# Hybrid attention layer on one core: earlier queries for the memory heads, halved loads for the sparse attention, a shorter preparation lead in the output product

## The chip, the core and the metric

The kernel runs on one core of a Trainium2 chip. The core has a matrix engine (TensorE, PE in the profile), VectorE (DVE), ScalarE (ACT), GpSimd (POOL), and SyncE (SP), whose queue issues the loads and stores. All five run their own list of instructions in order and wait for each other through semaphores; 16 DMA engines move data between main memory and the on-chip memory. The metric is the device time of one execution in microseconds (us).

## The reference

One layer on a sequence of 1024 tokens of width 2048. One projection feeds three groups of attention heads: multi-head latent attention (MLA, 8 heads), native sparse attention (NSA, 4 heads, with compressed, selected and window branches) and cross-attention to a memory of 256 tokens (4 heads). Everything is float32.

```python
def hybrid_layer(x, mem, cos, sin, norm_g, w_in, q_norm_g, w_uq, kv_norm_g, w_ukv,
                 cmp_pe_k, cmp_pe_v, cmp_w1k, cmp_w2k, cmp_w1v, cmp_w2v,
                 mem_norm_g, w_mem_kv, w_out):
    h = rmsnorm(x, norm_g) @ w_in
    offsets = np.cumsum(IN_SPLITS)[:-1].tolist()
    (c_q, c_kv, k_rope, z_mla, q_nsa, k_c, v_c, k_s, v_s, k_w, v_w, g_nsa, z_nsa,
     q_mem, z_mem) = jnp.split(h, offsets, axis=-1)
    o_mla = mla_mixer(c_q, c_kv, k_rope, cos, sin, q_norm_g, w_uq, kv_norm_g, w_ukv) * jax.nn.silu(z_mla)
    o_nsa = nsa_mixer(q_nsa, k_c, v_c, k_s, v_s, k_w, v_w, g_nsa,
                      cmp_pe_k, cmp_pe_v, cmp_w1k, cmp_w2k, cmp_w1v, cmp_w2v) * jax.nn.silu(z_nsa)
    o_mem = memory_mixer(q_mem, mem, mem_norm_g, w_mem_kv) * jax.nn.silu(z_mem)
    o = jnp.concatenate([o_mla, o_nsa, o_mem], axis=-1) @ w_out
    return x + o.astype(x.dtype)
...
    return rmsnorm(x, final_norm_g)
```

## The kernel before

Every float32 operand of the large products is split into a rounded high part and a remainder (`split`, L118 on ScalarE and L112 on VectorE), and `mm3` multiplies high by high, high by low and low by high (L124 to L126): three matmuls of 128x512 for one block.

**Stages.** Up to about 100 us the inputs are normalised. Up to 1000 us the projection runs: 40 units `u` of 7 products `s` each (a product scheme with 7 block products in place of 8), so products g = 7u + s; one product is 12 matmuls. After each product its bank is drained (`evac`), and from the second half on (u >= 20) GpSimd adds the first half's result with an accumulating DMA (work<-part). `post` finishes a unit: for the gate tiles a Silu on ScalarE (L795) and a store. From 1000 us come the four NSA heads (row blocks i = 0 to 7 of 128 tokens), up to about 1557 us the eight MLA heads, and then the output product and the final norm.

**Side work in the projection.** `at(u, s, f)` puts a piece of other work behind product (u, s): the compression of the NSA keys and values (chunks that pass through wh buffers), the memory heads (`mem_start`, `mem_scores`, ...) and, in unit 39, the loads for NSA (`nsa_keys`, `nsa_window`, `nsa_aux`, `nsa_values_in`, `nsa_masks`). There TensorE, VectorE, ScalarE and GpSimd keep the order of the program text; SP's order comes from a scheduler. In the NSA and MLA heads a scheduler orders all engines by priority.

**Memory heads.** Head h has its first scores at product 64 + 18h of the second half. `mem_start` (four products ahead) loads its queries (qh, ql: two wh buffers, 512 KB each) and its keys and values (km, vm into one rs buffer).

**Output product.** 56 products t of 24 matmuls, in seven phases p = t // 8 with k = t % 8. `w_load` and `a_load` bring weights (into a wraw buffer) and entries (ogT, into work buffers); `w_prep` splits the weights into a big buffer, `a_prep` adds or subtracts entries where the phase wants it (L1497, L1501) and splits the sum into a wh buffer. At the end of each phase `oevac` drains the eight PSUM banks into row buffers Y: on VectorE as sums (L1616 after the third phase, L1622 after the fourth). In phases 1, 3 and 5 the products go on in the banks of the phase before. `oside` does the residual, the squares of the norm (L1575), GpSimd's product with the norm's gain (L1651) and, in the last phase, row outputs: `inverse` (L1580 to L1587) and `scaled_out` (L1595 on VectorE). The last four products are done row by row, so that rows 4 to 7 can be finished one by one: there every row needs all of the four.

**Buffers.** big 16, wh 8, work 4, wraw 3, rs 2; PSUM banks S 4, T 2, O and J 2 together. In the output product gf, the eight Y and the four S1 and S2 hold 13 of the big buffers, so three are left for split weights. All of this part, from the gain's load on, keeps the order of the program text on the four engines:

```python
    for t in range(NT):
        p, k = divmod(t, 8)
        if t + 4 < NT:
            w_load(t + 4)
            a_load(t + 4)
        if t + 3 < NT:
            w_prep(t + 3)
            a_prep(t + 3)
```

Behind these lines stand the 24 matmuls of product t, then the drain where k is 7, then `oside(p, k)`.

Of the kernel before, what the change touches and what calls it, by code (L numbers as in the profile page):

```python
# [52 lines left out]
def hybrid_block_kernel(ctx: ExitStack, tc, a, out):  # L53
# [607 lines left out]
    mem = {}  # L661

    def mem_start(h):
        qh, ql = whl()
        load(f(qh), qmd[h][:, :1024])
        load(f(ql), qmd[h][:, 1024:])
        kv = rs()
# [4 lines left out]
        mem[h] = (qh, ql, kv)  # L672
# [115 lines left out]
    def post(u, n):  # L788
# [5 lines left out]
        elif j >= T_ZMLA:  # L794
            S.activation(o, o, AF.Silu)  # L795
# [198 lines left out]
    for h in range(4):  # L994
        g = 64 + 18 * h
        at(u0 + (g - 4) // 7, (g - 4) % 7, lambda h=h: mem_start(h))
# [9 lines left out]
    at(ul, 0, lambda: nsa_keys())  # L1006
    at(ul, 1, lambda: nsa_window())
    at(ul, 3, lambda: nsa_aux())
    at(ul, 4, lambda: nsa_values_in())
    at(ul, 6, lambda: nsa_masks())  # L1010

# [12 lines left out]
    def nsa_window():  # L1024
        kw = big()
        nsa["kwm"] = (kw[:, :1024], kw[:, 1024:])
        load(f(kw), kwd)
        kw = big()
        kw1, kw2 = nsa["kw"] = kw[:, :1024], kw[:, 1024:]
        for r0 in (0, 64):  # L1030
            load(f(kw1[r0:r0 + 64]), kswh[64:])
        load(f(kw2[:64]), kswl[64:])
        load(f(kw2[64:]), posd[:, 64:])

    def nsa_values_in():
        nsa["vs"], nsa["vw"] = big(), big()
        load(f(nsa["vs"]), vsd)
        load(f(nsa["vw"]), vwd)

    def nsa_keys():  # L1040

        kh, kl, k1, k2 = [slot() for _ in range(4)]
        nsa["ks"] = (kh, kl), k1, k2
        load(f(kh[:, :64]), kcd[:, :64])
        load(f(kl[:, :64]), kcd[:, 64:128])
        load(f(k1[:, :64]), kcd[:, 128:192])
        load(f(k2[:64, :64]), kcd[:64, 192:])
        load(f(kh[:, 64:]), ksd[:, :1024])
        load(f(kl[:, 64:]), ksd[:, 1024:])
        for r0 in (0, 64):  # L1050
            load(f(k1[r0:r0 + 64, 64:]), kswh[:64])
        load(f(k2[:64, 64:]), kswl[:64])
        load(f(k2[64:]), posd)
# [26 lines left out]
    post(2 * NU - 1, 0)  # L1080
    post(2 * NU - 1, 1)
# [326 lines left out]
    for h in range(4):  # L1408
        q = qn
        for i in range(8):  # L1410
# [5 lines left out]
            src = nsa_scores(h, q, i)  # L1416
            if h == 3 and i == 7:
                ckv.extend(latent(4))
# [68 lines left out]
    def a_prep(t, dst=None):  # L1487
# [8 lines left out]
        if p == 2:  # L1496
            V.tensor_tensor(s1, r[0], r[1], op=ALU.add)  # L1497
            V.tensor_tensor(s2, s1, r[2], op=ALU.subtract)
            src = s2
        elif p == 3:  # L1500
            V.tensor_tensor(r[0], r[0], r[1], op=ALU.subtract)  # L1501
            src = r[0]
        elif p == 4:
            src = s1
        elif p == 5:
            V.tensor_tensor(s2, r[0], s2, op=ALU.subtract)
            src = s2
        else:
            src = r[0]
# [306 lines left out]
```

## Time and profile before

| | us |
|---|---|
| three runs | 1887.09, 1892.62, 1897.51 |
| median | 1892.62 |
| the profiled execution | 1892.9 |
| its span, first to last instruction | 1891.1 |
| TensorE busy | 1786.8 (94%) |
| VectorE busy | 1317.0 (70%) |
| ScalarE busy | 854.9 (45%) |
| GpSimd busy | 323.8 (17%) |
| mean granted clock of TensorE | 0.979 |

A wait is given with the engine that idled, the line and tiles of the instruction that waited, and the instruction or transfer that came last by the profile. Where an instruction waits for several, the one named need not be the one that mattered. The granted clock is TensorE's share of full speed: 1.00 is 2.4 GHz, 0.50 is 1.2 GHz.

### The profile page before, as it was taken

How to read it: one execution, taken by the hardware profiler on the slowest of the kernel's cores; microseconds unless marked ns; L12 is line 12 of the kernel's file. 1: busy time of each engine (PE TensorE's matmuls, PEld its weight loads, DVE VectorE, ACT ScalarE, POOL GpSimd, SP SyncE). 2: the span in 40 equal slices, each digit the busy share in tenths (PEclk: the TensorE clock that was granted, in tenths of full speed). 3: DMA queues.
4: the chain of work that ended last, by engine and by line, in shares of the span. 5: the costliest groups of instructions: out<-in, count | busy, mean ns of one | idle time of the engine just before them, and what ended most of it. 6: DMA issues, size and time to landing. Idle time of an engine off the chain costs nothing. (4 is left out here: it accounts for less than half of the span.)

```text
span 1891.1 us, 26430 instructions
## 1 busy us (share of the span) xinstructions
PE 1786.8 (94%) x9294; PEld 1523.0 (81%) x9294; DVE 1317.0 (70%) x2478; ACT 854.9 (45%) x1712; POOL 323.8 (17%) x433
## 2 busy tenths in 40 slices
PE   8999999999999999999997999999999999989996
PEld 7888878887777777877776898888998988877885
DVE  7976878976866655666564887868778783454777
ACT  8754222222434344544555665545455453222344
POOL 0002322323233313233231222200000000000020
PEclk9999999999999999999998999999999999999998
DMA  6554877786678657978998233432122144654564
GB/s 220 187 189 165 286 263 267 253 298 237 225 211 255 161 173 231 293 214 243 307 265 242 68 97 109 167 114 62 46 77 64 57 154 150 226 167 145 172 194 191
DMA packets 124930, 351.91 MB, mean 186 GB/s; under 512 B 15355, under 2 KB 39613, under 8 KB 121725
## 3 DMA queue, kind: packets, MB, share of 16 engines
q1 hardware_dynamic: 119037, 329.25, 51.7%
q0 software_dynamic: 5760, 20.97, 6.3%
q8 instruction: 73, 1.20, 0.3%
q14 instruction: 60, 0.49, 0.1%
HBM read 242.14 MB, written 108.02 MB: 185 GB/s over the span
## 5 line engine op out<-in xcount | busy, mean ns | idle before, releaser
L124 PE MATMUL S<-big,wh 128*128 128x512 f32 x1336 | 528.7, 396 | 25.2 <-DVE work L772 8.3
L125 PE MATMUL S<-big,wh 128*128 128x512 f32 x1336 | 525.7, 393 | 4.4 <-DVE big L112 4.4
L126 PE MATMUL S<-big,wh 128*128 128x512 f32 x1336 | 525.3, 393 | 1.3 <-DVE wh L112 1.2
L124 PEld LDWEIGHTS S<-big,wh 128*128 128x128 f32 x1336 | 254.0, 190 | 82.0 <-issue 12.5
L125 PEld LDWEIGHTS S<-big,wh 128*128 128x128 f32 x1336 | 254.3, 190 | 56.7 <-DVE big L112 5.9
L126 PEld LDWEIGHTS S<-big,wh 128*128 128x128 f32 x1336 | 253.6, 190 | 56.9 <-DVE wh L112 3.0
L112 DVE TENSOR_TENSOR wh<-wraw,wh 128x512 fp32r<-128x512 f32 (+2 forms) x226 | 199.0, 882 | 73.8 <-ACT wh L118 73.6
L118 ACT ACTIVATE wh<-wraw 128x512 fp32r<-128x512 f32 (+2 forms) x226 | 145.4, 659 | 90.4 <-PE S L126 44.2
L112 DVE TENSOR_TENSOR big<-wraw,big 128x1024 fp32r<-128x1024 f32 x56 | 73.9, 1320 | 105.1 <-ACT big L118 100.5
L733 POOL TENSOR_TENSOR wraw<-wraw 128x512 f32<-128x512 f32 x38 | 56.6, 1488 | 459.6 <-DMA wraw<-in_w_feat 394.6
L659 ACT ACTIVATE work<-S,st 128x512 f32<-128x512 f32 (+3 forms) x148 | 84.6, 573 | 86.5 <-DVE st L1114 35.1
L118 ACT ACTIVATE wh<-rs 128x512 fp32r<-128x512 f32 x80 | 50.2, 628 | 157.7 <-POOL rs L734 125.6
L112 DVE TENSOR_TENSOR wh<-rs,wh 128x512 fp32r<-128x512 f32 x80 | 63.0, 787 | 65.5 <-ACT wh L118 65.4
L118 ACT ACTIVATE big<-wraw 128x1024 fp32r<-128x1024 f32 x56 | 59.2, 1056 | 85.6 <-PE J L126 59.4
L124 PE MATMUL J<-big,wh 128*128 128x512 f32 x214 | 84.1, 393 | 0.8 <-ACT wh L118 0.7
L125 PE MATMUL J<-big,wh 128*128 128x512 f32 x214 | 84.0, 393 | 0.0
L126 PE MATMUL J<-big,wh 128*128 128x512 f32 x214 | 83.9, 392 | 0.0
L118 ACT ACTIVATE wh<-T 128x512 fp32r<-128x512 f32 (+2 forms) x112 | 53.0, 504 | 45.6 <-PE T L1179 29.5
L770 ACT ACTIVATE work<-S 128x512 f32<-128x512 f32 x40 | 23.9, 597 | 106.7 <-PE S L126 99.2
L112 DVE TENSOR_TENSOR wh<-T,wh 128x512 fp32r<-128x512 f32 (+2 forms) x112 | 61.5, 569 | 10.6 <-ACT wh L118 10.3
L1443 POOL MEMSET wh<- 128x128 f32 x64 | 13.8, 228 | 291.8 <-PE O L125 173.6
L1096 PE MATMUL S<-big,big 128*128 128x512 f32 (+2 forms) x144 | 52.9, 367 | 9.7 <-ACT wraw L659 9.7
(378 smaller groups left out, 4132.1 us busy)
## 6 DMA issues: line engine op xcount, KB each, us to landing
wraw<-in_w_feat SPq DMA_DIRECT2D x80, 512.0 KB, 5.5
part<-work SPq DMA_DIRECT2D x40, 512.0 KB, 3.7
work<-part POOLq DMA_DIRECT2D x40, 512.0 KB, 6.4
work<-og SPq DMA_DIRECT2D x72, 256.0 KB, 4.0
wh<-in_w_o SPq DMA_DIRECT2D x32, 512.0 KB, 7.2
t<-wh SPq DMA_DIRECT2D x32, 512.0 KB, 3.0
wraw<-t SPq DMA_DIRECT2D x32, 512.0 KB, 3.7
wraw<-in_w_o SPq DMA_DIRECT2D x24, 512.0 KB, 3.9
```

Of the source, the lines that this page charges most:

```text
L112: V.tensor_tensor(dst, src, f(hi), op=ALU.subtract)
L118: S.activation(hi, src, AF.Copy)
L124: PE.matmul(dst, sh, mh, start=start, stop=False, skip_group_check=shared)
L125: PE.matmul(dst, sh, ml, start=False, stop=False, skip_group_check=shared)
L126: PE.matmul(dst, sl, mh, start=False, stop=stop, skip_group_check=shared)
L659: S.activation(dst, src, AF.Exp, bias=m, scale=-1.0, accum_out=s)
L733: E.tensor_tensor(B12, B22, B12, op=ALU.subtract)
L770: S.activation(C21, B, AF.Copy)
L1096: PE.matmul(d, qm[0][:, c:c + P], km[0][:, k0:k0 + n], start=True, stop=False)
L1443: G.memset(f(t[:, o:o + P]), 0.0)
```

## The change

1. The memory heads' query loads move from four to eight products ahead of the head's first scores; keys and values stay at four (`mem_kv`).
2. The loads for NSA are split into two halves of columns and begin two products earlier; the masks (cmask, cm01, vc) and their copy come behind the first half of the keys and ahead of the window. All second halves come last.
3. The Silus of the last unit leave the end of the projection and stand in NSA head 0 behind the scores of blocks 1 and 2, at that place of ScalarE's order.
4. In the output product, weights and entries are split two products ahead in place of three; entries are still added up three ahead (`a_sum` and `a_split` in place of `a_prep`).
5. In the third phase (p = 2) the low halves of rows 0 to 3 are squared and multiplied by the gain; in the last phase only the high half is squared, and the low half's scaling is done on ScalarE.

The diff, cut to its core:

```diff
     def mem_start(h):
...
+        mem[h] = qh, ql
+
+    def mem_kv(h):
         kv = rs()
...
-        mem[h] = (qh, ql, kv)
+        mem[h] += kv,
...
-    def post(u, n):
+    def post(u, n, pin=False):
...
-            S.activation(o, o, AF.Silu)
+            x = S.activation(o, o, AF.Silu)
+            if pin:
+                tc.keep_in_program_order(x)
             store(zd[j - T_ZMLA], o)
...
-        at(u0 + (g - 4) // 7, (g - 4) % 7, lambda h=h: mem_start(h))
+        at(u0 + (g - 8) // 7, (g - 8) % 7, lambda h=h: mem_start(h))
+        at(u0 + (g - 4) // 7, (g - 4) % 7, lambda h=h: mem_kv(h))
...
-    at(ul, 0, lambda: nsa_keys())
-    at(ul, 1, lambda: nsa_window())
-    at(ul, 3, lambda: nsa_aux())
-    at(ul, 4, lambda: nsa_values_in())
-    at(ul, 6, lambda: nsa_masks())
+    at(ul - 1, 6, lambda: nsa_keys(0))
+    at(ul, 0, lambda: nsa_aux())
+    at(ul, 1, lambda: nsa_window(0))
+    at(ul, 3, lambda: nsa_values_in(0))
+    at(ul, 5, lambda: nsa_masks(), lambda: nsa_keys(1), lambda: nsa_window(1), lambda: nsa_values_in(1))
...
+    def nsa_window(n):
+        if n == 0:
+            nsa["w"] = big(), big()
+        km, kr_ = nsa["w"]
...
+        c = slice(512 * n, 512 * n + 512)
+        load(halves(f(km))[:, :, c], halves(kwd)[:, :, c])
         for r0 in (0, 64):
...
+            load(f(kw1[r0:r0 + 64, c]), kswh[64:, c])
+        load(f(kw2[:64, c]), kswl[64:, c])
+        load(f(kw2[64:, c]), posd[:, 64 + 512 * n:576 + 512 * n])
...
-    post(2 * NU - 1, 0)
-    post(2 * NU - 1, 1)
...
             src = nsa_scores(h, q, i)
+            if h == 0 and i in (1, 2):
+                post(2 * NU - 1, i - 1, True)
...
-    def a_prep(t, dst=None):
+    asrc = {}
+
+    def a_sum(t):
...
+    def a_split(t, dst=None):
         e = slot()[:, :1024] if dst is None else dst
-        split(e[:, :512], e[:, 512:], src)
+        split(e[:, :512], e[:, 512:], asrc.pop(t))
         ent[t] = e
...
+        if p == 2 and k < 4:
+            square(Y[k][:, L_], st_(k, 0))
+            G.tensor_tensor(Y[k][:, L_], Y[k][:, L_], gf[:, L_], op=ALU.mult)
...
             if k < 4:
-                square(Y[k][:, L_], st_(k, 0))
                 square(Y[k][:, H_], st_(k, 1))
             if 0 < k <= 4:
                 r = inverse(k - 1, 2)
-                scaled_out(k - 1, r, L_)
+                scaled_out(k - 1, r, L_, True)
                 scaled_out(k - 1, r, H_)
...
+        if t + 2 < NT:
+            w_prep(t + 2)
+            a_split(t + 2)
         if t + 3 < NT:
-            w_prep(t + 3)
-            a_prep(t + 3)
+            a_sum(t + 3)
```

What moves on the engines is shown at three places. The first is ScalarE where NSA begins. A line number is followed by the operation, what it writes and what it reads; wraw with st is an exponential's result with its sum, rs from wraw is the copy of the masks, work from work a Silu. Before:

```order
L659 ACT_TABLE_LOAD
L659 ACTIVATE wraw_8102,st_8100<-S_8109,st_8100 128x128
L1063 ACTIVATE rs_8040<-wraw_8041 128x576
L795 ACT_TABLE_LOAD
L795 ACTIVATE work_7965<-work_7965 128x1024
L795 ACTIVATE work_7966<-work_7966 128x1024
L659 ACT_TABLE_LOAD
L659 ACTIVATE wraw_8102,st_8100<-S_8103,st_8100 128x64
```
In the changed kernel, behind the head's first eight exponentials (L798 is a Silu, L1175 the scaling of a branch, L118 a split):

```order
L1175 ACTIVATE wraw_8142<-wraw_8142,st_8140 128x256
L798 ACT_TABLE_LOAD
L798 ACTIVATE work_7980<-work_7980 128x1024
L118 ACTIVATE big_8170<-T_8174 128x3x128
L659 ACT_TABLE_LOAD
L659 ACTIVATE wraw_8182,st_8180<-S_8189,st_8180 128x384
L118 ACTIVATE big_8170<-O_8210 128x4x128
L118 ACTIVATE big_8171<-T_8217 128x128
L1175 ACTIVATE wraw_8182<-wraw_8182,st_8180 128x384
L798 ACT_TABLE_LOAD
L798 ACTIVATE work_7981<-work_7981 128x1024
L659 ACT_TABLE_LOAD
```
Each Silu went behind exponentials of head 0 and has a table load on either side: four behind the first exponential, where there were two. The masks' copy (now L1081) stands ahead of the first exponential and its table.

The second is VectorE at the end of the third output phase, around the first two of the eight sums of the drain (L1616, in the changed kernel L1639; big from wraw is the weights' subtraction of one product, wh from work that of its entries). Before:

```order
L112 TENSOR_TENSOR big_15586<-wraw_15545,big_15586 128x1024
L1501 TENSOR_TENSOR work_15547<-work_15547 128x512
L112 TENSOR_TENSOR wh_15590<-work_15547,wh_15590 128x512
L112 TENSOR_TENSOR big_15622<-wraw_15581,big_15622 128x1024
L1501 TENSOR_TENSOR work_15583<-work_15583 128x512
L112 TENSOR_TENSOR wh_15626<-work_15583,wh_15626 128x512
L1616 TENSOR_TENSOR big_15068<-big_15022,S_15357 128x512
L1616 TENSOR_TENSOR big_15138<-big_15023,S_15358 128x512
```
In the changed kernel:

```order
L112 TENSOR_TENSOR big_15606<-wraw_15528,big_15606 128x1024
L112 TENSOR_TENSOR wh_15609<-work_15530,wh_15609 128x512
L1521 TENSOR_TENSOR work_15567<-work_15567 128x512
L112 TENSOR_TENSOR big_15642<-wraw_15565,big_15642 128x1024
L112 TENSOR_TENSOR wh_15645<-work_15567,wh_15645 128x512
L1521 TENSOR_TENSOR work_15603<-work_15603 128x512
L1639 TENSOR_TENSOR big_15076<-big_15030,S_15365 128x512
L1639 TENSOR_TENSOR big_15146<-big_15031,S_15366 128x512
```
Before, the last weights ahead of the drain are those of the product three ahead (big_15622, t = 26 while t = 23 runs); in the changed kernel they are those of t = 25 (big_15642), and for t = 26 only the entries' subtraction stands there.

The third is ScalarE in the tail, up to the weights of the last product, t = 55 (big from wraw and wh from work are the splits of its weights and entries; st from st is a row's square root, work with st a row's square). Before:

```order
L1575 ACTIVATE work_16740,st_14726<-big_15293 128x1024
L1582 ACTIVATE st_14726<-st_14726 128x1
L118 ACTIVATE big_16754<-wraw_16704 128x1024
L118 ACTIVATE wh_16757<-work_16706 128x512
L1582 ACTIVATE st_14726<-st_14726 128x1
L1575 ACTIVATE work_16797,st_14727<-big_15022 128x512
```
In the changed kernel (L1616 is now a row's scaling):

```order
L1605 ACTIVATE st_14740<-st_14740 128x1
L1616 ACTIVATE big_15219<-big_15219,st_14740 128x1024
L118 ACTIVATE big_16766<-wraw_16670 128x1024
L118 ACTIVATE wh_16769<-work_16672 128x512
L1605 ACTIVATE st_14740<-st_14740 128x1
L1616 ACTIVATE big_15301<-big_15301,st_14740 128x1024
L118 ACTIVATE big_16784<-wraw_16718 128x1024
L118 ACTIVATE wh_16787<-work_16720 128x512
L1598 ACTIVATE work_16815,st_14741<-big_15030 128x512
```
Ahead of the last product's splits stand now the square roots of rows 2 and 3 and the scalings of both, where the last one was row 2's square root.

## Rows read from the trace of the kernel before

**Rows 1.** Waits of TensorE, 995 to 1030 us: total us, times, longest.
```profile
PE S L1096 <- ACT wraw L659: 11.8, 2, 9.7
PE S L1100 <- DMA big<-pos: 1.2, 1, 1.2
```
**Rows 2.** Windows: length; busy us (instructions) of PE, PEld, DVE, ACT, POOL; PEclk, DMA share, GB/s.
```profile
925.00:930.00 5.00, 1.87 (x9) 1.44 (x8) 3.41 (x4) 2.86 (x3) 0.00 (x0) 0.84 1.05 332
1000.00:1005.00 5.00, 3.12 (x22) 2.63 (x20) 1.05 (x3) 0.28 (x1) 2.12 (x7) 1.00 1.04 289
1020.00:1025.00 5.00, 5.00 (x24) 4.65 (x24) 3.15 (x11) 3.58 (x11) 1.47 (x6) 0.60 0.27 102
1645.00:1665.00 20.00, 20.00 (x90) 16.57 (x89) 7.37 (x11) 4.97 (x6) 0.00 (x0) 1.00 0.53 178
1685.00:1705.00 20.00, 14.87 (x54) 11.74 (x54) 9.82 (x14) 3.84 (x5) 0.00 (x0) 0.83 0.38 114
1733.00:1757.00 24.00, 19.98 (x83) 16.11 (x82) 15.89 (x21) 6.65 (x9) 0.00 (x0) 0.93 0.34 100
```
**Rows 3.** Timeline of ScalarE at NSA's start: start, length, instruction, [idle before <-releaser].
```profile
1011.63 0.68 ACT L1063 ACTIVATE rs<-wraw 128x576 fp32r<-128x576 f32 x1 [5.15 <-DMA wraw<-in_cm]
1012.33 1.28 ACT L795 ACT_TABLE_LOAD   x1
1013.63 2.00 ACT L795 ACTIVATE work<-work 128x1024 f32<-128x1024 f32 x2
...
1016.94 0.31 ACT L659 ACTIVATE wraw<-S,st 128x64 f32<-128x64 f32 x1
...
1024.42 0.29 ACT L659 ACTIVATE wraw<-S,st 128x64 f32<-128x64 f32 x1
```
**Rows 4.** DMA issues, 996 to 1003 us: count, KB each, median us to landing.
```profile
work<-part POOLq DMA_DIRECT2D x2, 512.0 KB, 9.5
...
wraw<-in_cm SPq DMA_DIRECT2D x1, 32.0 KB, 14.7
```
**Rows 5.** Timeline of TensorE, the waits around the memory heads.
```profile
731.42 0.33 PE L124 MATMUL J<-wh,dh 128*66 128x256 f32 x1 [1.70 <-ACT wh L118]
...
867.65 0.36 PE L124 MATMUL J<-rs,wh 128*128 128x256 f32 x1 [2.34 <-DMA z<-z]
...
927.54 0.39 PE L124 MATMUL J<-rs,wh 128*128 128x256 f32 x1 [2.30 <-DMA wh<-qm]
...
928.86 0.58 PE L126 MATMUL J<-rs,wh 128*128 128x256 f32 x1 [0.82 <-DMA wh<-qm]
```
**Rows 6.** Waits of TensorE in the output product, 1557 to 1885 us.
```profile
PE S L124 <- DVE big L1616: 5.1, 1, 5.1
PE S L124 <- DVE big L1622: 4.0, 1, 4.0
PE S L125 <- DVE big L112: 3.4, 2, 2.6
PE S L124 <- ACT wh L118: 1.4, 1, 1.4
```
**Rows 7.** Timeline of VectorE at the end of the third phase.
```profile
1686.60 1.23 DVE L112 TENSOR_TENSOR big<-wraw,big 128x1024 fp32r<-128x1024 f32 x1 [2.21 <-ACT big L118]
...
1689.73 2.48 DVE L1616 TENSOR_TENSOR big<-big,S 128x512 f32<-128x512 f32 x4
```
**Rows 8.** Timeline of SP's queue: head 3's query loads.
```profile
920.64 1.21 SPq L102 DMA_DIRECT2D wh<-qm  x2
```
**Rows 9.** Timeline of GpSimd at the end of the sixth phase.
```profile
1835.01 2.41 POOL L1651 TENSOR_TENSOR big<-big,big 128x1024 f32<-128x1024 f32 x1 [11.78 <-ACT work L1575]
```
**Rows 10.** Timeline of VectorE in the last phase: splits of four products' weights.
```profile
1835.92 2.59 DVE L112 TENSOR_TENSOR big<-wraw,big 128x1024 fp32r<-128x1024 f32 x1 [2.22 <-ACT big L118]
...
1852.67 1.22 DVE L112 TENSOR_TENSOR big<-wraw,big 128x1024 fp32r<-128x1024 f32 x1
...
1858.38 1.22 DVE L112 TENSOR_TENSOR big<-wraw,big 128x1024 fp32r<-128x1024 f32 x1
```

More of the change, by code (lines that the diff above doesn't have):

```diff
@@ L1022, in nsa_q @@
         return (q[:, :1024], q[:, 1024:]), q1, q2
[L1024 to L1029, printed above, removed]
-        for r0 in (0, 64):
[L1031 to L1049, printed above, removed]
+    def halves(t):
+        return t.rearrange("p (t c) -> p t c", t=2)
+    def nsa_window(n):
+        if n == 0:
+            nsa["w"] = big(), big()
+        km, kr_ = nsa["w"]
+        nsa["kwm"] = (km[:, :1024], km[:, 1024:])
+        kw1, kw2 = nsa["kw"] = kr_[:, :1024], kr_[:, 1024:]
+        c = slice(512 * n, 512 * n + 512)
+        load(halves(f(km))[:, :, c], halves(kwd)[:, :, c])
+        for r0 in (0, 64):
+            load(f(kw1[r0:r0 + 64, c]), kswh[64:, c])
+        load(f(kw2[:64, c]), kswl[64:, c])
+        load(f(kw2[64:, c]), posd[:, 64 + 512 * n:576 + 512 * n])
@@ new lines, in nsa_values_in, with nsa_keys @@
+    def nsa_values_in(n):
+        if n == 0:
+            nsa["vs"], nsa["vw"] = big(), big()
+        c = slice(512 * n, 512 * n + 512)
+        load(halves(f(nsa["vs"]))[:, :, c], halves(vsd)[:, :, c])
+        load(halves(f(nsa["vw"]))[:, :, c], halves(vwd)[:, :, c])
+    def nsa_keys(n):
+        if n == 0:
+            kh, kl, k1, k2 = [slot() for _ in range(4)]
+            nsa["ks"] = (kh, kl), k1, k2
+            load(f(kh[:, :64]), kcd[:, :64])
+            load(f(kl[:, :64]), kcd[:, 64:128])
+            load(f(k1[:, :64]), kcd[:, 128:192])
+            load(f(k2[:64, :64]), kcd[:64, 192:])
+            load(f(k2[64:, :64]), posd[:, :64])
+        (kh, kl), k1, k2 = nsa["ks"]
+        c, d = slice(512 * n, 512 * n + 512), slice(64 + 512 * n, 576 + 512 * n)
+        load(f(kh[:, d]), ksd[:, c])
+        load(f(kl[:, d]), ksd[:, 1024 + 512 * n:1536 + 512 * n])
@@ L1050, in nsa_keys @@
         for r0 in (0, 64):
-            load(f(k1[r0:r0 + 64, 64:]), kswh[:64])
-        load(f(k2[:64, 64:]), kswl[:64])
-        load(f(k2[64:]), posd)
+            load(f(k1[r0:r0 + 64, d]), kswh[:64, c])
+        load(f(k2[:64, d]), kswl[:64, c])
+        load(f(k2[64:, d]), posd[:, d])
     def nsa_aux():
@@ L1520, in o_first @@
             w_prep(t)
-            a_prep(t, e[:, t * 1024:t * 1024 + 1024])
+            a_sum(t)
+            a_split(t, e[:, t * 1024:t * 1024 + 1024])
     d, own = lat_pieces(0, None)
@@ L1664, in hybrid_block_kernel @@
         a_load(t)
-    w_prep(2)
-    a_prep(2)
+    a_sum(2)
     for t in range(NT):
```

10 lines of the change are left out of this document (5 added, 5 removed).

## Prediction, made before the changed kernel was run

> **What bounds the kernel now.** I read the page first (busy time by engine), then the waits of TensorE, then windows and timelines around its longest waits, and last the timelines of the engine that each wait names. TensorE is busy 94% of 1891.1 us. The diff leaves its matmuls as they are, so the 104 us of idle time, and the matmuls that run at 1.2 GHz behind a long gap, are all that can be won. The change touches four places where TensorE waits.
>
> *Entry of the sparse attention (NSA), from 1000 us:* TensorE is idle 11.8 us for exponentials of ScalarE and 1.2 us for the window's keys [rows 1]. The granted clock is still 0.60 from 1020 to 1025, though TensorE is busy all the while [rows 2]. ScalarE waits 5.15 us for in_cm, copies it, changes its table, does two Silus, changes back, and only at 1016.94 does the compressed scores' exponential [rows 3]. in_cm took 14.7 us to land [rows 4], for the whole window stands ahead of it in SP's queue.
>
> *Memory heads 2 and 3:* TensorE waits 2.34 us at 867.65, then 2.30 and 0.82 us near 928 [rows 5]. The last two name the query load. The first names a z load, but that matmul reads only rs and wh; I read it as the head's keys, which stand behind its queries on the queue.
>
> *Output product:* after its third and its fourth phase TensorE waits 5.1 and 4.0 us for VectorE's bank sums, L1616 and L1622 [rows 6]. VectorE isn't slow there: ahead of the sums stands L112, 2.21 us late for ScalarE's split of a product three ahead [rows 7], and that split needs the big buffer of the product that TensorE is just finishing. Other phase ends show no such wait.
>
> *Tail:* 3.4 and 1.4 us of waits for the splits of the last products [rows 6].
>
> **Part by part.** *NSA entry.* The loads are halved, the masks go ahead of the window, the two Silus behind the scores of blocks 1 and 2. By the tile sizes in the diff, the window's first half has 2.4 MB up to its end in place of 4.0 MB, and in_cm 1.3 MB in place of 4.9 MB. At 289 GB/s [rows 2] in_cm lands 12.4 us earlier, near 999, and the window near 998: neither is waited for. A microsecond of scores, VectorE's minimum and one table load of 1.28 us [rows 3] then put the compressed scores' exponential near 1002.8 (an estimate), 14.1 us before 1016.94. But each Silu now costs table, Silu, table on the engine that sets the pace here: 1.28 + 1.00 + 1.28 = 3.56 us, twice 7.1. From 1016.94 to block 3's first exponential at 1024.42 ScalarE took 7.5 us [rows 3]; after, 1002.8 + 7.5 + 7.1 = 1017.4. Gain 7.0. Lower bound: if only the window's 2 MB count (7.1 us), in_cm lands at 1004.5, copy and table put the exponential at 1006.5, and 3.3 is left. Upper bound: if the Silus fall where ScalarE idles, the 13.0 us of [rows 1] go.
>
> *Memory heads.* Two query loads of 512 KB go four products (10.9 us) earlier; keys and values stay. Head 3's queries were issued at 920.64 [rows 8], 6.9 us before the matmul that waited for them; with 10.9 us more they have 17.8, above any latency in [rows 4]. Head 2's keys lose 1 MB straight ahead of them, 3.6 us at 289 GB/s, more than the wait of 2.34. Gain: 5.5 us of idle time, and I put the clock of 0.84 around the second gap [rows 2] at 1.5 us: 7.0. Bounds: 3.1 (head 3's idle time alone) to 7.6. Head 0's queries now hold two of the eight wh slots while the compression's chunks pass through them. The nearest wait there is one of 1.70 us [rows 5]; I take 0.5 us lost, with bounds of 0 and 3.
>
> *Output phases.* Preparing t+2 in place of t+3 needs the buffer of product t-1, free when product t starts, so nothing that waits for product t stands ahead of the sums. A bank is complete after its own part of the last product, so the first sums run while the last banks fill. Both gaps go. Full speed is 90 matmuls in 20 us [rows 2]; 1685 to 1705 has 54, so 36 x 0.222 = 8.0 us are lost, and 1733 to 1757 has 83 of 108, 5.6 us lost [rows 2]. Gain 13.6; lower bound 9.1, the idle time alone. What hides the later preparation: its chain of two splits and two subtractions, none over the 1.23 us of L112 [rows 7], is under 4.9 us, the lead of two products 10.9 us.
>
> *Third phase.* Four squares of ScalarE and four products of GpSimd (2.41 us [rows 9]) move here, where VectorE is busy 7.37 and ScalarE 4.97 of 20 us [rows 2]. L112 beside such a product took 2.59 us in place of 1.22 [rows 10]: 1.4 us four times, within the slack. I take 0, and a bound of 2 lost, in which the tighter work buffers are. The Trainium skill (SBUF — State Buffer, "Who interferes with whom") calls the ports that VectorE shares with GpSimd an exclusive lock; the row shows 1.37 us lost of 2.41. By the page each of the four could cost VectorE the whole 2.41, 9.6 us in all, and the sum would stay as it is, since the slack covers that too.
>
> *Tail.* The split of the last product stood behind the outputs of rows 0 to 2; now it stands behind row 3's too. A step of row outputs takes 5.71 us on VectorE [rows 10]. After, VectorE does one product less in a step, but ScalarE's scaling, of about the length of a split, comes ahead of the next weight split: factor, scaling, split, subtraction, factor become a ring of 5.5 us (an estimate from 5.71). One step more, less the subtraction of 1.22 us that no longer precedes the first step and 0.2 us in each of the others: 5.5 - 1.2 - 0.4 = 3.9, so the last L112, started at 1858.38 [rows 10], starts 4 us later in its phase. TensorE waits for it: 4.0 lost. Bounds: nothing, if the ring starts sooner by the squares taken away, to 8, with half clock behind the longer gap.
>
> *Sum:* 7.0 + 7.0 - 0.5 + 13.6 - 4.0 = 23.1 us. The profiled execution took 1892.9 us (its span 1891.1); less 23.1 that is 1869.8. The median of the runs, 1892.62, is 0.3 us lower, so I predict 1869.5.
>
> **Rivals.** (a) *The Silus eat the entry.* Each Silu also needs the accumulating transfer of its tile; two issued as the stage begins took 9.5 us [rows 4], so about 1009 and 1011, when ScalarE reaches them. If each holds ScalarE for 2 us, the entry gains 3; with the memory heads at 4 and the tail at its 4 lost: 1892.9 - 3 - 4 - 13.6 + 4.5 = 1876.8. For it: four table loads between exponentials where two were. Against it: the DMA queue empties sooner. (b) *All gaps go and the tail loses nothing:* 13 + 7.5 + 13.6 = 34, 1859. Against it: two table loads more on ScalarE, the engine that sets the pace [rows 3]. (c) *The halved loads lose rate.* All these bytes had landed by 1020 before (DMA share 0.27 then [rows 2]); block 4, near 1018 in my forecast, is the first to read the second halves. If they come 10 us after it, the entry loses 3: 1892.9 - 23.1 + 10 = 1879.8. The Trainium skill (DMA: Bandwidth & Descriptors, "Measured (HBM→SBUF, 128 partitions, SWDGE, issued from GpSimd)") asks for 1 MiB and more in a transfer and calls those under 64 KB dominated by descriptors; no run so far has these tiles halved. (d) *Slower: the shorter lead becomes a wait of every product.* Preparation of t+2 starts when t-1 ends; each of some 46 products waits by what its chain takes beyond 10.9 us. The rows give under 4.9, and 9.9 with eight bank sums ahead (four take 2.48 [rows 7]). If a sum of ogT entries, which waits for its loads in VectorE's order, held it to 11.7, 46 x 0.8 = 37 us: 1906. Against it: a DMA share of 0.53 in the third phase [rows 2], where the most entries are loaded. (e) *At the phase ends the change doesn't do what it says:* another buffer is short, the sums still wait, 13.6 is 0: 1883.4.
>
> **How the numbers follow.** Forecast (1864 to 1874): 0.50. (a) 0.17, (b) 0.13, (c) 0.06, (d) 0.05, (e) 0.09. The range 1859 to 1881 leaves out (d), (e) and some of (b), together 0.2; its ends are those of (b) and (c) with a microsecond for the terms not in them. 0.5% (9.5 us) is about what a measurement of this kernel can tell from no change. Under 1883.1, faster by more: the forecast, (a), (b), (c) and a third of (e), 0.88; within it 0.08; slower 0.04.
>
> **What would show it.** In the profile after: the compressed scores' exponential near 1003, no wait for in_cm, the Silus apart, block 3 some 7 us earlier; no TensorE wait on wh<-qm; none on the bank sums after phases three and four, where VectorE starts summing before the product ends; in the tail a longer wait for the last L112. Wrong would be idle time of TensorE in every product of the output (d), block 4's scores waiting for a transfer (c), or ScalarE waiting for the accumulating transfers (a).

## The result: 0.9905 of the time before, where the forecast was 0.988

| | us | of before |
|---|---|---|
| before, median of 4 runs | 1892.11 | |
| changed, median of 4 runs (1871.36 to 1878.71) | 1876.63 | 0.9905, 95% interval 0.9879 to 0.9931 |
| forecast | 1869.5 (1859 to 1881) | |
| changed, the profiled execution; its span | 1875.79; 1874.0 | |

Both kernels issue the same matmuls, so the two traces can be laid over each other: I counted TensorE's matmuls of 128x512 into the S banks, took the start of each from the timelines, and read by how much the same matmul comes later or earlier than in the trace of before. The differences of these numbers say where time went or came from; a stretch's own number is how much its end moved against its start.

| stretch (times of before) | forecast | changed less before, us |
|---|---|---|
| start to 835 (normalisation, projection, vc chunks, heads 0 and 1) | +0.5 | +4.3 |
| 835 to 981 (memory heads 2 and 3) | -7.0 | -2.0 |
| 981 to 1500 (NSA entry, NSA heads, most of the MLA heads) | -7.0 | -5.8 |
| 1500 to 1566 (the last MLA heads) | 0 | -2.7 |
| end of the third output phase | -8.0 | -8.1 |
| end of the fourth | -5.6 | -5.7 |
| tail, to the last matmul | +4.0 | +3.0 |
| sum | -23.1 | -17.0 |

**NSA entry.** What answers to [rows 1], TensorE's waits from 995 to 1030 us in the changed kernel (total us, times, longest):

```profile
PE S L1112 <- ACT wraw L659: 4.3, 3, 2.8
PE S L1112 <- ACT work L659: 1.1, 1, 1.1
```
And what answers to [rows 3], ScalarE's timeline (start, length, instruction, idle before and releaser):

```profile
1003.62 0.32 ACT L659 ACTIVATE wraw<-S,st 128x64 f32<-128x64 f32 x1 [6.79 <-DVE st L1245]
...
1009.93 1.28 ACT L798 ACT_TABLE_LOAD   x1
1011.23 1.06 ACT L798 ACTIVATE work<-work 128x1024 f32<-128x1024 f32 x1
...
1012.68 1.28 ACT L659 ACT_TABLE_LOAD   x1
...
1016.58 1.28 ACT L798 ACT_TABLE_LOAD   x1
1017.87 1.06 ACT L798 ACTIVATE work<-work 128x1024 f32<-128x1024 f32 x1
1018.95 1.28 ACT L659 ACT_TABLE_LOAD   x1
1020.25 0.31 ACT L659 ACTIVATE wraw<-S,st 128x64 f32<-128x64 f32 x1
```
11.8 and 1.2 us of waits became 4.3 and 1.1; four further waits of 0.3 to 0.7 us, 1.9 us in all, stand in the new trace, where before had one of 0.3. NSA's first matmul begins at 1002.4 in this trace, the first compressed exponential follows 1.2 us later (the table has been loaded ahead), and block 3's stands at 1020.25, 17.9 us behind that matmul, where the forecast had 17.3 and before had 24.3. Between them stand the two excursions as priced: 1009.93 to 1013.98 and 1016.58 to 1020.25, with 3.6 us of tables and Silu in each.

The 2.7 us from 1500 to 1566 are not the entry's. All of them come up between 1540 and 1557 (1536 to 1551 in the new trace), in code that the change leaves alone, and go with TensorE's clock. Before, then changed (length; busy us and instructions of PE, PEld, DVE, ACT, POOL; clock, DMA share, GB/s):

```profile
1540.00:1560.00 20.00, 17.02 (x87) 14.68 (x88) 17.15 (x38) 12.70 (x26) 0.00 (x0) 0.83 0.60 195
1536.00:1556.00 20.00, 16.31 (x97) 13.59 (x97) 18.44 (x39) 12.78 (x26) 0.00 (x0) 1.00 0.65 210
```
The granted clock is 0.83 and 1.00 over these 20 us. Before, it is 0.60 from 1543 to 1547 and 0.57 from 1553 to 1557, in part at 1.2 GHz, behind waits of TensorE of 0.7, 0.5 and 0.3 us and of 0.5 and 1.0 us; in the new trace, behind waits of 0.2 to 1.4 us, it stays at 2.4 GHz. Two runs described below with before's loads for NSA, a_only and silu_only, also have 1.00 there and gain 2.0 and 2.7 us, and two with the whole of the changed NSA part, e_undone and rows_later, have 0.83 and gain 0.05. So this part of the difference is luck.

**Memory heads.** Neither head waits for its queries or keys any more, but TensorE does wait at head 3:

```profile
937.42 0.79 PE L124 MATMUL S<-big,wh 128*128 128x512 f32 x1 [4.07 <-ACT work L773]
```
The 4.07 us are in no row of before. ScalarE's timeline there, VectorE's one row ahead of it, and the windows (columns as above; the last two are of the output phases, below):

```profile
931.18 1.06 ACT L118 ACTIVATE big<-big 128x1024 fp32r<-128x1024 f32 x1 [5.94 <-DMA z<-z]
...
936.77 0.59 ACT L773 ACTIVATE work<-S 128x512 f32<-128x512 f32 x1
```
```profile
929.82 1.28 DVE L628 SCALAR_TENSOR_TENSOR big<-big,kvg 128x1024 f32<-128x1024 f32 x1 [3.25 <-DMA big<-r]
```
```profile
920.00:925.00 5.00, 4.30 (x20) 3.27 (x19) 3.32 (x4) 2.55 (x5) 2.89 (x2) 1.00 1.06 402
925.00:930.00 5.00, 5.00 (x26) 4.25 (x25) 1.47 (x3) 0.24 (x1) 0.88 (x1) 1.00 1.04 411
930.00:935.00 5.00, 3.35 (x15) 2.44 (x13) 3.83 (x5) 2.86 (x3) 0.00 (x0) 1.00 1.05 310
935.00:940.00 5.00, 2.58 (x6) 2.10 (x7) 3.36 (x7) 3.18 (x8) 3.78 (x3) 0.60 1.00 306
1675.00:1700.00 25.00, 25.00 (x112) 20.68 (x112) 16.84 (x23) 6.85 (x10) 0.00 (x0) 1.00 0.55 185
1720.00:1745.00 25.00, 25.00 (x112) 20.72 (x111) 18.66 (x23) 8.30 (x11) 0.00 (x0) 1.00 0.54 168
```
VectorE's L628 rescales a tile of the latent; it waited 3.25 us for that tile's load and ended at 931.10. ScalarE's split of it waited until 931.18 (its row names z<-z, but it reads what L628 wrote), and behind it in ScalarE's order stand head 3's exponentials and at 936.77 the drain of a bank (L773) that TensorE needs. The DMA share is 1.00 to 1.06 in the four windows from 920 to 940. The load was issued at 921.47, 8.4 us before L628 began; before, at 918.83, 6.6 us before it. TensorE's clock is 0.60 around its wait, and the drain costs 6.9 us against the trace of before, more than the 4.07 of the wait.

**Output phases.** What answers to [rows 7], VectorE at the end of the third phase:

```profile
1675.03 1.23 DVE L112 TENSOR_TENSOR big<-wraw,big 128x1024 fp32r<-128x1024 f32 x1 [3.01 <-ACT big L118]
...
1677.38 2.47 DVE L1639 TENSOR_TENSOR big<-big,S 128x512 f32<-128x512 f32 x4
...
1682.16 1.22 DVE L112 TENSOR_TENSOR big<-wraw,big 128x1024 fp32r<-128x1024 f32 x1
```
The sums follow the entries' subtraction without a gap, and the next weights' L112 comes behind them. The windows around both phase ends (the last two above, 1675 to 1700 and 1720 to 1745) show TensorE busy throughout, with 112 matmuls in 25 us at clock 1.00; no wait answers to L1616 and L1622 of [rows 6].

**Tail.** TensorE's waits, and the L112 that answer to [rows 10]:

```profile
1835.71 0.50 PE L124 MATMUL S<-big,wh 128*128 128x512 f32 x1 [2.74 <-ACT wh L118]
1836.45 0.50 PE L125 MATMUL S<-big,wh 128*128 128x512 f32 x1 [0.24 <-DVE big L112]
...
1841.21 0.80 PE L124 MATMUL S<-big,wh 128*128 128x512 f32 x1 [3.37 <-ACT wh L118]
```
```profile
1835.17 1.23 DVE L112 TENSOR_TENSOR big<-wraw,big 128x1024 fp32r<-128x1024 f32 x1 [0.90 <-ACT big L118]
...
1840.67 1.23 DVE L112 TENSOR_TENSOR big<-wraw,big 128x1024 fp32r<-128x1024 f32 x1 [0.90 <-ACT big L118]
```
6.35 us of waits against 4.8 [rows 6], one 5.5 us step of the row outputs after the other, and the last L112, at 1840.67, 2.3 us later than before's 1858.38 when both are counted from the fourth phase's end (20.0 us apart by then). The waits are 1.55 us more of the 3.0 lost; most of the rest is clock, here over the same 12 us of before and of the changed kernel:

```profile
1855.00:1867.00 12.00, 7.95 (x26) 5.94 (x26) 10.10 (x22) 3.10 (x7) 0.00 (x0) 0.72 0.45 177
1835.00:1847.00 12.00, 7.58 (x16) 4.71 (x17) 6.64 (x13) 4.20 (x8) 0.00 (x0) 0.59 0.45 175
```

### The profile page after: what moved, and what is told of

Its sections match the earlier page's. It is cut to its first block, busy times and chain, and to the rows that moved or that the text cites. A ratio compares the mean times of both kernels' runs of the same rounds, so it can differ in the third digit from the quotient of the medians.

```text
span 1874.0 us, 26480 instructions
## 1 busy us (share of the span) xinstructions
PE 1784.2 (95%) x9294; PEld 1519.3 (81%) x9294; DVE 1313.3 (70%) x2474; ACT 860.9 (46%) x1718; POOL 332.2 (18%) x437
## 4 chain that ended last, share of the span: by engine, by line
PE 44%; DVE 4%; ACT 3%; issue 2%; DMA 2%; POOL 1%; SPq 0%; DVEq 0%; ACTq 0%; POOLq 0%
PE S L124 4%; PE S L125 4%; PE S L126 4%; PE J L124 3%; PE J L125 3%; PE J L126 3%; PE O L125 3%; PE O L124 3%; PE O L126 3%; PE T L1195 2%; PE S L1112 2%; PE S L1113 1%; PE S L1116 1%; PE S L1115 1%; PE S L1114 1%
## 5 line engine op out<-in xcount | busy, mean ns | idle before, releaser
L112 DVE TENSOR_TENSOR wh<-wraw,wh 128x512 fp32r<-128x512 f32 (+2 forms) x226 | 197.7, 876 | 77.4 <-ACT wh L118 77.4
L118 ACT ACTIVATE wh<-wraw 128x512 fp32r<-128x512 f32 (+2 forms) x226 | 145.6, 658 | 94.9 <-PE S L126 44.2
L112 DVE TENSOR_TENSOR big<-wraw,big 128x1024 fp32r<-128x1024 f32 x56 | 78.2, 1396 | 92.4 <-ACT big L118 89.1
L118 ACT ACTIVATE wh<-rs 128x512 fp32r<-128x512 f32 x80 | 50.2, 628 | 160.5 <-POOL rs L737 127.5
L112 DVE TENSOR_TENSOR wh<-rs,wh 128x512 fp32r<-128x512 f32 x80 | 63.5, 794 | 64.6 <-ACT wh L118 64.4
L118 ACT ACTIVATE big<-wraw 128x1024 fp32r<-128x1024 f32 x56 | 59.2, 1057 | 92.7 <-issue 42.3
L118 ACT ACTIVATE wh<-T 128x512 fp32r<-128x512 f32 (+2 forms) x112 | 53.1, 504 | 42.8 <-PE T L1195 28.6
L773 ACT ACTIVATE work<-S 128x512 f32<-128x512 f32 x40 | 23.9, 596 | 103.2 <-PE S L126 99.0
L112 DVE TENSOR_TENSOR wh<-T,wh 128x512 fp32r<-128x512 f32 (+2 forms) x112 | 61.5, 569 | 9.3 <-ACT wh L118 9.1
L1195 PE MATMUL T<-ident,work 128*128 128x128 f32 x383 | 58.9, 274 | 1.8 <-DVE wh L112 1.4
```

The source lines that it names most:

```text
L112: V.tensor_tensor(dst, src, f(hi), op=ALU.subtract)
L118: S.activation(hi, src, AF.Copy)
L773: S.activation(C21, B, AF.Copy)
L1195: PE.transpose(T[:, t * P:t * P + P], blocks[i + t][1], ident)
```

## Experiments

Each was executed once, with a profile, and read with the same overlay of matmuls, unless a ratio with its interval is given. "Stage" means the stretch from 981 to 1500, "memory heads" that from 835 to 981, "tail" from the last whole products to the last matmul, all against the first trace of before. The kernel before took 1894.84 us when it ran beside the first four kernels, 1898.79 beside the next four, and 1894.83 (median of 8) beside rows_later, best and changed_again; these differ by more than some of the effects, and so the verdicts go by the stretches.

### The query loads alone (a_only)

```diff
         load(f(ql), qmd[h][:, 1024:])
+        mem[h] = qh, ql
+
+    def mem_kv(h):
         kv = rs()
...
-        at(u0 + (g - 4) // 7, (g - 4) % 7, lambda h=h: mem_start(h))
+        at(u0 + (g - 8) // 7, (g - 8) % 7, lambda h=h: mem_start(h))
+        at(u0 + (g - 4) // 7, (g - 4) % 7, lambda h=h: mem_kv(h))
```

> The kernel before with part 1 alone: the memory heads' queries loaded eight products ahead, all else as before. Theory 1 (the DMA queue is full from about 905 to 937 us, so the megabyte of queries only makes the tiles behind it late): the waits on the queries go (2.3 us at head 2, 3.1 us and 0.8 us of half clock at head 3), and a new wait of about 4 us comes at head 3, where ScalarE stands at the split of a rescaled latent tile (L118 behind L628) and the drain of a bank (L770) stands behind it. Net about 2 us faster than before, near 1890. Rival 1 (the new wait comes from the earlier NSA loads or another part): no wait on the drain at head 3, some 6.4 us faster, near 1886.

Measured: 1892.39 us. TensorE's waits from 730 to 1035 us:

```profile
PE S L1100 <- ACT wraw L659: 11.6, 2, 9.4
...
PE S L124 <- ACT work L773: 3.6, 1, 3.6
```
The waits on queries and keys are gone, and the wait on the drain (L773) is there without any other part of the change. The memory heads are 3.6 us shorter: 2.6 at head 2; at head 3 4.6 saved, 5.5 lost to the drain, and 2.0 gained behind it. So the new wait belongs to the moved queries, and rival 1 falls.

### The query loads put back (a_undone)

```diff
-        at(u0 + (g - 8) // 7, (g - 8) % 7, lambda h=h: mem_start(h))
+        at(u0 + (g - 4) // 7, (g - 4) % 7, lambda h=h: mem_start(h))
```

> The changed kernel with the query loads back at four products ahead, all else as changed. Theory 1: both waits on the queries and keys return (2.3 and 3.1 us) and the 4 us wait of TensorE on the drain at head 3 goes, so the time is within 3 us of the changed kernel's 1876.6, near 1878.6. Rival 1: the waits return and the wait on the drain stays, 6.4 us more, near 1883.

Measured: 1882.07 us, nearer to rival 1's time than to theory 1's. Waits of TensorE:

```profile
PE J L124 <- DMA wh<-qm: 4.1, 1, 4.1
...
PE J L124 <- DMA rs<-km: 3.3, 1, 3.3
...
PE J L126 <- DMA wh<-qm: 2.8, 1, 2.8
```
The wait on the drain is gone and those on the loads are back, as theory 1 has it and rival 1 does not. But they are longer than in the trace of before (4.1, 3.3 and 2.8 us against 2.30, 2.34 and 0.82 [rows 5]), and the memory heads are 5.8 us longer than there, not equal. Up to there the code, and SP's order of transfers, are the same as before's, so here the same loads landed later. Here the wait at head 2 names rs<-km, the keys, which was my reading of the row that named z<-z.

### The latent's tiles later (c_late)

```diff
-    for j, (u, t) in enumerate(((9, 2), (9, 6), (10, 3), (15, 1), (15, 5), (16, 2), (16, 6), (17, 3))):
+    for j, (u, t) in enumerate(((9, 2), (9, 6), (10, 3), (15, 1), (15, 5), (16, 3), (17, 1), (17, 6))):
         at(u0 + u, t, lambda j=j: c_load(j))
-        x = 7 * (u0 + u) + t + 3
+        x = 7 * (u0 + u) + t + (3 if j < 4 else 4)
```

> The changed kernel, where the last three latent tiles are loaded one to three products later and rescaled four products after their load in place of three. Theory 1: the 4.07 us wait on the drain at head 3 goes, and nothing comes in its place, 4.4 us less than the changed kernel, near 1872. Rival 1 (the wait is of another tile or of the wh buffers): it stays, near 1876.6.

Measured: 1880.04 us. The wait on the drain is gone, as theory 1 has it: by 960 us heads 2 and 3 have gained 7.8 us. But "nothing comes in its place" was wrong. 4.3 of the 7.8 are lost again between 960 and 981. TensorE's waits from 730 to 1035 us:

```profile
PE T L1195 <- ACT wraw L1175: 4.7, 2, 3.7
...
PE S L1116 <- DMA big<-pos: 2.3, 1, 2.3
...
PE S L1112 <- DMA big<-kw: 0.6, 1, 0.6
...
PE S L1115 <- DMA big<-kswh: 0.3, 1, 0.3
```
Three of the rows now name transfers of the window (kw, kswh, pos), and TensorE stands at the entry: the stage lost its whole gain (2.5 us longer than before's, where the changed kernel has -5.8), and the time is not better. The window's first kw load is issued at 994.22, against 991.47 in the changed kernel, though TensorE is 4.4 us ahead of it at the stage's start; the DMA share is 0.94 to 1.03 from 975 to 1005. That the later tiles are what held the window back is my reading and not shown: SP's order changed in more than these tiles, for the masks are issued at 969.63, in the changed kernel at 989.03.

### The sums ahead of the preparation (drain_first)

```diff
-        if t + 2 < NT:
-            w_prep(t + 2)
-            a_split(t + 2)
-        if t + 3 < NT:
-            a_sum(t + 3)
+        if k < 7:
+            prep(t + 3)
...
                     oevac(p, i, j)
+        if k == 7:
+            prep(t + 3)
         oside(p, k)
```

(prep does the weights, the sum and the split of one product.)

> The changed kernel with weights and entries prepared three products ahead again, as before, but at the end of each output phase the eight bank sums are written ahead of the preparation. Theory 2 (the waits at the phase ends came from the order of VectorE's instructions alone, not from a lead of three): no wait on the sums, 0 us lost at both phase ends; and the tail's loss of 3.0 us against before is taken back, since the last product's split stands behind the outputs of rows 0 to 2 again: near 1873.6. Rival 2 (a lead of three is itself too tight, by buffers): waits of 5.1 and 4.0 us at the phase ends return, near 1887.

Measured: 1875.66 us, 8.1 and 5.7 us gained at the two phase ends, within 0.02 us of those of the changed kernel, and a tail 0.1 us longer than before's in place of 3.0. So the phase ends waited for VectorE's order alone; a lead of three products is enough, and the shorter lead bought nothing but the tail's loss. Its tail:

```profile
1836.94 0.49 PE L124 MATMUL S<-big,wh 128*128 128x512 f32 x1 [1.22 <-ACT wh L118]
1837.68 0.49 PE L125 MATMUL S<-big,wh 128*128 128x512 f32 x1 [0.25 <-DVE big L112]
...
1842.45 0.80 PE L124 MATMUL S<-big,wh 128*128 128x512 f32 x1 [3.67 <-ACT wh L118]
```
(1.22, 0.25 and 3.67 us, against the 6.35 of the changed kernel.) The sum doesn't show the gain of 2.9 us since this execution was slower elsewhere.

### The Silus back, the loads kept (silu_back), and the Silus moved alone (silu_only)

```diff
-            if h == 0 and i in (1, 2):
-                post(2 * NU - 1, i - 1, True)
...
+    post(2 * NU - 1, 0)
+    post(2 * NU - 1, 1)
```

> The changed kernel with the last unit's two Silus back at the end of the projection, ahead of the sparse attention's first exponential; the halved and reordered loads stay. Theory 3 (the loads alone don't free the entry, since the Silus wait for their accumulating transfers until about 1009 and 1011 us): the second Silu ends near 1012, table and first compressed exponential near 1013.5, block 3's exponential 7.5 us later, near 1021 counted from a stage start at 1000, so of the entry's 8.4 us gain about 3 are left and the kernel takes about 1882. Rival 3 (the Silus' place does not matter once the masks are early): the stage keeps its 8.4 us, near 1876.6.

Measured: 1887.24 us, the stage 0.2 us longer than before's. ScalarE's timeline:

```profile
1014.42 1.28 ACT L798 ACT_TABLE_LOAD   x1 [7.46 <-DMA work<-part]
...
1018.18 1.06 ACT L798 ACTIVATE work<-work 128x1024 f32<-128x1024 f32 x1 [1.41 <-DMA work<-part]
```
The masks are early, but now the Silu stands ahead of everything and waits 7.46 us for the accumulating transfer of its tile, and the second one 1.41 us. Before, the wait for in_cm hid this wait. I had expected 3 us left of the gain; nothing was.

silu_only is the kernel before with the same lines the other way round: out of the end of the projection, into NSA head 0.

> The kernel before with the two Silus moved behind the scores of blocks 1 and 2, and its loads as before. Theory 3: in_cm still lands near 1011.6, so the compressed exponential starts near 1013.7 in place of 1016.94, and each Silu costs table, Silu, table (3.56 us) behind it: block 3's exponential near 1028 in place of 1024.4, the stage 2 to 4 us longer, near 1895. Rival 3: the move itself is what pays, the stage 3 us or more shorter, 1889 or less.

Measured: 1904.33 us, the stage 5.3 us longer than before's, more than the 2 to 4 expected. (8.8 us lie ahead of the stage, in code that is before's, and 2.7 come back from 1500 to 1566 with the clock.)

```profile
1015.00 1.28 ACT L659 ACT_TABLE_LOAD   x1 [13.80 <-DVE st L1114]
...
1021.10 0.68 ACT L1065 ACTIVATE rs<-wraw 128x576 fp32r<-128x576 f32 x1 [4.35 <-DMA wraw<-in_cm]
```
in_cm still lands late, and nothing of the head can pass its copy; the exponentials behind it then pay for the tables. So neither of the two parts alone gains anything (0.2 and 5.3 us lost), and both together gain 5.8: each removes one of two waits that ended at about the same time.

### Both Silus together (silu_pair)

```diff
-            if h == 0 and i in (1, 2):
-                post(2 * NU - 1, i - 1, True)
+            if h == 0 and i == 2:
+                post(2 * NU - 1, 0, True)
+                post(2 * NU - 1, 1, True)
```

> The changed kernel with both Silus together behind the scores of block 2: two table loads of 1.28 us less on ScalarE. Theory 4 (ScalarE sets the pace at the stage's start, so its table loads count in full): the stage from 1000 to the output product is 2.6 us shorter, near 1874. Rival 4 (the table loads fall where ScalarE would wait anyway): no change in the stage, within 0.5 us.

Measured: 1869.68 us, the stage 11.4 us shorter than before's, 5.6 more than the changed kernel in its first trace.

```profile
1011.54 1.28 ACT L798 ACT_TABLE_LOAD   x1
1012.84 2.00 ACT L798 ACTIVATE work<-work 128x1024 f32<-128x1024 f32 x2
1014.86 1.28 ACT L659 ACT_TABLE_LOAD   x1
```
Two loads of 1.28 us are gone. The stage's gain in the two traces with the pair, 11.4 and 8.5 us (in best, below), lies above all six with the Silus apart and the loads as changed, 4.7 to 6.1; so rival 4 falls, though the spread is too wide to say that it is 2.6 us and no more. The pair also puts the first Silu one block later; no run tells that from the two table loads. TensorE's next wait there seems to be for a transfer, 3.4 us for vs:

```profile
PE S L1112 <- DMA big<-vs: 3.4, 1, 3.4
```
But in best the same matmul waits as long, and the row names ScalarE's exponential behind the two Silus:

```profile
1021.66 0.58 PE L1112 MATMUL S<-wh,big 128*128 128x256 f32 x1 [3.36 <-ACT work L659]
```
In both traces it starts 0.15 us after that exponential's end. So ScalarE ends this wait too, and vs only landed at about the same time.

### Part 5 undone (e_undone)

```diff
-        if p == 2 and k < 4:
-            square(Y[k][:, L_], st_(k, 0))
-            G.tensor_tensor(Y[k][:, L_], Y[k][:, L_], gf[:, L_], op=ALU.mult)
...
             if k < 4:
+                square(Y[k][:, L_], st_(k, 0))
                 square(Y[k][:, H_], st_(k, 1))
...
-                scaled_out(k - 1, r, L_, True)
+                scaled_out(k - 1, r, L_)
```

> The changed kernel without part 5: the low halves of rows 0 to 3 are squared in the last phase again and scaled on VectorE with the gain, no GpSimd product in the third phase. Theory 5 (the tail's 3.0 us loss comes from the shorter lead, which puts row 3's output ahead of the last split; part 5 makes that smaller): the loss grows to 5 or 6 us, since four more squares of 1.04 us and 0.2 us more per step stand ahead: near 1879. Rival 5 (the scaling on ScalarE, ahead of the weight split, is the loss): the tail is back at the level of before, near 1873.6.

Measured: 1882.83 us; the tail is 6.0 us longer than before's, against 3.0 in the changed kernel and 0.1 in drain_first. So the shorter lead costs the tail 6 us, and with it part 5 takes 3 of them back; rival 5 falls. With a lead of three, as in drain_first, part 5 gives the tail nothing (0.1 us longer than before's).

### Rows put out one product later (rows_later), and the three edits together (best)

```diff
-            if 0 < k <= 4:
-                r = inverse(k - 1, 2)
-                scaled_out(k - 1, r, L_, True)
-                scaled_out(k - 1, r, H_)
+            if 1 < k <= 5:
+                r = inverse(k - 2, 2)
+                scaled_out(k - 2, r, L_, True)
+                scaled_out(k - 2, r, H_)
```

> The kernel of drain_first (three products ahead, sums first at the phase ends), where in the last phase the outputs of rows 0 to 3 also stand one product later each, so that the last product's split stands behind the outputs of rows 0 and 1 only. Theory 5 (the last split is late by the row outputs ahead of it, 5.5 us each): TensorE's waits in the tail (4.8 us in the kernel before) go, and with the clock that comes back the time from the fourth phase's end to the last matmul is 5 to 8 us shorter than in the kernel before. Rival 5b (the splits are late by their weights' loads or buffers): the waits stay and that stretch is within 1 us of before.

Measured: 1871.93 us, and the tail 2.8 us shorter than before's, little more than half of the least that I expected. One wait of TensorE is left:

```profile
1838.45 0.74 PE L124 MATMUL S<-big,wh 128*128 128x512 f32 x1 [3.05 <-ACT wh L118]
```
It is ScalarE's split again (L118): one output fewer stands ahead of the last split, two still do. That the outputs are the cause holds; the size didn't, since I had counted all waits as gone.

> The changed kernel with three edits: both Silus together behind block 2 (as in silu_pair), three products ahead with the sums first at the phase ends (as in drain_first), and rows 0 to 3 put out one product later. If the three are independent: 4.0 us (stage of silu_pair) + 3.0 us (tail of drain_first) + 5 us (rows_later) less than the changed kernel's 1876.6, near 1865; if the row outputs only move the end of VectorE's work, 5 us more.

Measured in five executions beside five of the changed kernel on the same chip: 1867.59 us, 0.9855 of before (95% interval 0.9833 to 0.9876), where the changed kernel has 1874.60 us and 0.9888 (0.9869 to 0.9907). 2.6 us short of the expectation: in its trace the stage is 8.5 us shorter and the tail only 1.3, where rows_later has 2.8 with the same code. Both have the same single wait (3.04 us in best and 3.05 in rows_later); what differs is the clock behind it, in rows_later and in best:

```profile
1838.00:1848.00 10.00, 9.55 (x34) 7.27 (x35) 7.89 (x23) 4.70 (x10) 0.00 (x0) 0.83 0.71 279
1836.30:1846.30 10.00, 9.56 (x27) 7.11 (x28) 7.89 (x23) 4.67 (x10) 0.00 (x0) 0.66 0.71 279
```

### Both kernels once more (changed_again, before_again)

> The changed kernel once more, for the same chip and rounds as best: 0.988 to 0.993 of before, and, stage by stage, the same 8.13 and 5.72 us at the phase ends and the 3 us lost in the tail; the parts up to the last output phases that hang on a full DMA queue (memory heads) may differ by some us from the first execution.

Measured: 1874.60 us (1870.11 to 1876.78). The phase ends give 8.1 and 5.7 us again, the tail costs 2.5, the stage gains 6.1 (and 1.7 come behind it, to 1566), the memory heads 3.8, with 3.9 us of wait on the drain; up to 835 us it is 0.1 us from the first trace of before, where the first trace of the changed kernel was 4.3.

> The kernel before once more, unchanged, for a second trace of it. If the waits of the memory heads hang on how the transfers of that moment fall (theory 1), the stretch from 835 to 981 us is some us longer than in the first trace, as in the two kernels that have the same code there (a_undone 5.8, silu_only 4.6 us); if the first trace is typical, within 1 us of it. The stretches of the output product up to the tail repeat to 0.1 us.

Measured: 1896.34 us. Waits of TensorE from 855 to 990 us:

```profile
PE J L124 <- DMA wh<-qm: 2.7, 1, 2.7
...
PE J L124 <- DMA rs<-km: 1.9, 1, 1.9
PE J L126 <- DMA wh<-qm: 1.1, 1, 1.1
```
The memory heads are 0.35 us from the first trace of before, so that one was typical of this kernel, the second of the two cases above. Up to 835 us it is 3.7 us later.

## Why the prediction was right, and where it was off

The direction and the range held; the median missed the forecast by 7.1 us, and the profiled execution the sum by 6.0. Two parts of the measured difference are not the change's, 4.3 us lost up to 835 us and 2.7 gained from 1500 to 1566; that they partly cancel is luck. By its own steps:

- **Output phases: right in mechanism and size.** 13.6 forecast, 13.86 measured, in every trace that has either order. The drain_first run adds what I had not seen: the lead was not needed, only the order.
- **NSA entry: right in mechanism, 1.2 us less than forecast.** 7.0 forecast, 5.8 up to 1500 us in the first trace; 6.1 in the second, and 4.7 to 6.1 over six traces. The terms can be read off: the exponential comes 1.2 us behind NSA's first matmul (2.7 forecast), the Silus take 7.2 us. That neither part alone gains anything was not said; the prediction priced them as one sum, and the runs show that it must be one.
- **Third phase: right, nothing.** From 1566 to 1680 us the two traces keep their distance to 0.01 us, with four squares and four GpSimd products more. The Trainium skill (SBUF — State Buffer, "Who interferes with whom") has an exclusive lock there, and the trace agrees: the four L112 that began beside these products (at 1641.06, 1647.84, 1653.28 and 1658.91) took 2.58, 1.75, 2.26 and 2.57 us in place of 1.22, each longer by what was left of its product (1.50, 0.67, 1.17, 1.50 us) less 0.13 to 0.15. These 4.3 us stayed inside the slack, as the prediction said by either price.
- **Tail: right in mechanism, 3.0 lost where 4.0 was forecast** (2.0 to 3.0 over six traces). The ring of 5.5 us came as estimated; the last L112 is 2.3 us later, not 4, and the lower clock adds to it. e_undone shows the two terms apart: +6.0 for the lead, -3.0 for part 5.
- **Memory heads: the step that failed.** 7.0 forecast, 2.0 measured; 0.9 to 3.8 over nine traces with the early queries and the latent's tiles in their place, each with a wait of 3.6 to 5.7 us on the drain. Head 2 gave its 2.6. At head 3 the prediction took 10.9 us of lead to be enough and didn't ask what the same megabyte delays and what is late next: the latent's tile behind it on a full queue, its split on ScalarE, and the drain behind that. a_only shows the new wait with this part alone, c_late that it goes when the tiles are moved. In the trace of before it was covered, since TensorE stood at the queries until 928.86 anyway. The vc slots, 0.5 us forecast, can't be told from the variation.
- **Up to 835 us: not in the sum.** 4.3 us more than in the first trace of before, in code that the change barely touches. Over the other 13 traces of this study that stretch lies 0.1 to 7.0 us above the first trace, 3.7 us for the kernel before itself: the trace that I started from was the fastest of all there. I took the difference of 0.3 us between the profiled execution and the median as the whole of the uncertainty, and it is not.

Of the rivals, (a) has the time that came out, 1876.8, but not for its reason: no Silu of the changed kernel waited for its transfer (in silu_back they did, for 7.46 us). (d) and (e) did not come. (c) did not come in the changed kernel: in its second trace a row names the window's kw for 2.75 us, but in the first the same matmul waits 2.76 us and the row names ScalarE. The Trainium skill (DMA: Bandwidth & Descriptors, "Measured (HBM→SBUF, 128 partitions, SWDGE, issued from GpSimd)") asks for 1 MiB and more, which the whole tiles of kw and vs had (1024 KB) and their halves have not; no run here has the new order of the loads with whole tiles, so what the halving itself costs is not shown.

What stays open: why the kernels that load the queries late spend 0.0 and -0.4 us in the memory heads in the two traces of before but 4.6 and 5.8 us in silu_only and a_undone, whose code there is the same. SP's order of transfers is the same too. That loads land differently is seen; what sets it was not tried. Nor was what sets the clock from 1540 to 1557.

## What to carry to other kernels

Before a load is moved ahead on a queue that the windows show full, name the transfers that it passes: the time saved at one consumer can be lost at the next one, and a wait that ends at about the same time as the one removed is not in the trace of before. Where two causes end a wait together, cost their removal as one edit; alone each may lose. And where an engine works in program order, put the short step that another engine waits for ahead of the one that itself waits: that needed no shorter lead, and kept the tail. Before a gain is put down to a change, look where in the trace it comes up: 2.7 us of this one came 500 us behind the place that was changed.

## What the runs showed of the hardware

Transfers issued in one order land differently: the same code in the memory heads took 0.35 us less to 5.8 us more than in the first trace of before, in before_again and a_undone, while what the output phases gained repeated to 0.03 us. A change of ScalarE's table cost 1.28 us and the next instruction began 0.02 us later (1018.95 to 1020.25); the two Silus together, with two changes less, gave a stage 2.4 to 6.7 us shorter than the six traces with the Silus apart.

TensorE's clock can differ where the work does not: behind one wait of the same length (3.05 and 3.04 us) the mean over 10 us was 0.83 in one run and 0.66 in another, 1.5 us of difference in the tail. And a VectorE subtraction of two inputs in SBUF that begins beside a GpSimd product waits out most of what is left of it: it took 0.53 to 1.36 us longer where 0.67 to 1.50 us of the product were left.
